# Gate/up products: a fourth of eight steps by sevens, and residual additions on GpSimd

## The chip, the cores and the metric

The kernel runs on one core of a Trainium2 chip. The metric is the device time of one execution in microseconds (us), and the median of several runs is compared. Engines are named as in the profile: PE (TensorE, matrix products; PEld is its weight load), DVE (VectorE), ACT (ScalarE), POOL (GpSimd) and SP (the queue that issues the loads).

## The reference

A two-layer decoder trunk on one sequence of 256 tokens with 2048 features. The first layer mixes tokens by causal pooling, the second by differential attention; each is followed by a SwiGLU feed-forward part with 5632 inner features. Cut to the part that the change touches:

```python
def swiglu(h, wg, wu, wd):
    return (jax.nn.silu(h @ wg) * (h @ wu)) @ wd

for i in range(DEPTH):
    hn = rmsnorm(h, norm_mix[i])
    mix = pool_mixer(...) if i % 2 == 0 else diff_attention(...)
    h = h + mix
    h = h + swiglu(rmsnorm(h, norm_ffn[i]), w_gate[i], w_up[i], w_down[i])
return rmsnorm(h, final_norm)
```

Everything is float32.

## The kernel before, in words

**A product as three.** Every float32 operand is split into a high half (a cast to the matrix type) and a low half (the rest). A product is then three matrix products of 128x128 by 128x512: high by high, high by low, low by high (lines 178 to 181).

**Groups and steps.** The 256 tokens are two blocks of 128 rows, and the weights come in groups of two column blocks of 512. A group runs over the contracted dimension in steps of 256 (two blocks of 128). So one step multiplies a 2x2 grid of blocks by a 2x2 grid of blocks. In the plain way that takes eight block products, 24 matrix products, into four banks of PSUM (C11, C12, C21, C22, which are banks M2, P3, P4 and X). In the way *by sevens* (Strassen's scheme as Winograd wrote it) it takes seven block products, 21 matrix products, into the banks M1, M2, M6, M7, P5, P3 and P4. Which of a group's steps go by sevens is written in constants: SEVEN for gate/up, SEVEN_DOWN for the down product, SEVEN_QKV and SEVEN_O for attention (lines 40 to 43). A gate/up group has eight steps, of which SEVEN names three.

**What a step costs the other engines.** `load` (L107) brings 128x2048 float32 of weights, 1 MB, through SP's queue into one of three buffers `raw`. `halves` (L112) makes `whi` (ACT) and `wlo` (DVE), of which there are three buffers as well; a step by sevens leaves out the block that it doesn't use as it is, so they are 128x1536. For a step by sevens `sums` (L119) also makes four sums of weight blocks in `tsum` (three DVE instructions), and `sum_halves` (L127) their halves `thi` (ACT) and `tlo` (DVE). Of `tsum`, `thi` and `tlo` there is one buffer each.

**Recombination.** After a group with steps by sevens, `combined` (L195) turns the eight banks into four blocks in SBUF: two ACT copies (L201, of M1, and L205, of P5) and eight DVE instructions.

**The feed-forward part.** `ffn` (L443) takes the 11 gate/up groups in chunks of 4, 4 and 3. After each gate/up group come SiLU (L463) and the product with the up half (L464), and two calls of `pair` (L245), which transpose the result block by block on PE into a bank and split it into halves, an `h` tile each. A tile for a step by sevens needs eight blocks (four of them sums, L264 to L268), an ordinary one four. After a chunk come two down groups (o = 0 and 1) over the `h` tiles of the chunk, whose result is added to the residual `x_tok` (L487, four DVE instructions of 128x512 a group). In the first layer, group 0 has one step by sevens alone.

**Banks.** There are eight. `aux` (L79) hands out banks 0 to 3 in turn for transposes; banks 4 to 7 are C12/P3, C21/P4, C11/M2 and C22/X.

**What sets the order.** The program is written as a sequence; a planner orders each engine's instructions before the run, by their place in the sequence (the priority) and by its own estimate of when operands and buffers come free. On the chip each engine goes through its list in order and waits on semaphores. The pool `hp` belongs to one layer's feed-forward part, `resid` and `const` to the whole kernel.

Of the kernel before, what the change touches and what calls it, by code (L numbers as in the profile page):

```python
# [39 lines left out]
SEVEN = (2, 4, 6)  # L40
SEVEN_DOWN = (2, 4, 6)
SEVEN_QKV = (4, 6)
SEVEN_O = (6,)

# [8 lines left out]
def trunk_kernel(ctx, tc, x_n, gains, scale_in, final_in, subln, lam_in, band, dist,  # L53
# [19 lines left out]
    turn = {"aux": 0, "of": 4}  # L73

    def bank(i, shape=(P, 512)):
        return psum.tile(list(shape), F32, name=f"b{i}", tag=f"b{i}")

# [7 lines left out]
    dist_sb = const.tile([P, 2 * P], F32, name="dist_sb")  # L85
    ident = const.tile([P, P], F32, name="ident")
    ones = const.tile([P, P], F32, name="ones")
    nc.vector.memset(ones, 1.0)
    make_identity(nc, ident)

# [9 lines left out]
    def tile_of(xp, k):  # L100
        return xp[k // 2][:, k % 2]

# [35 lines left out]
    def group(steps, pool, by_bank=0):  # L138
# [14 lines left out]
        ps = {}  # L153
# [9 lines left out]
        def products(a, seven, w, b, parts):  # L163
            first = b not in ps
            if first:
                ps[b] = bank(b)
            for at, which, block in parts:
                hi, lo = w[which]
                if seven:
                    ah, al = a[:, 0, at], a[:, 1, at]  # L170
                else:
                    k, t = at
                    if a.shape[2] == 8:
                        slot = ((A11, A21), (A12, A22))[k][t]
                        ah, al = a[:, 0, slot], a[:, 1, slot]
                    else:
                        ah, al = (a[:, k, i, t * P:(t + 1) * P] for i in range(2))
                for x, y in ((ah, hi), (ah, lo), (al, hi)):
                    left[b] -= 1
                    nc.tensor.matmul(ps[b], x, y[:, block], start=first, stop=(left[b] == 0))  # L180
                    first = False
# [13 lines left out]
    def combined(ps, pool):  # L195
# [4 lines left out]
        m1, u2, u3, p5 = (pool.tile([P, 512], F32, name=f"c{i}") for i in ("11", "12", "21", "22"))  # L200
# [44 lines left out]
    def pair(dst, src, gains, seven):  # L245

        ps = aux((P, 2, 2, P))
# [14 lines left out]
        for i, at in ((0, slice(A21, A11 + 1)), (1, slice(A22, A12 + 1, A12 - A22))):  # L262
            nc.scalar.activation(e[:, at], ps[:, i], AF.Copy, scale=1.0 if gains is None else gains[i])
        nc.vector.tensor_tensor(e[:, S1:S3 + 1], e[:, A21:A11 + 1], e[:, A22:A21 + 1], ALU.subtract)  # L264
        nc.vector.tensor_tensor(e[:, S2], e[:, S1], e[:, A11], ALU.subtract)
        nc.vector.tensor_tensor(e[:, S4], e[:, A12], e[:, S2], ALU.add)
        nc.scalar.copy(dst[:, 0], e)
        nc.vector.tensor_tensor(dst[:, 1], e, f32(dst[:, 0]), ALU.subtract)  # L268
# [11 lines left out]
    with tc.tile_pool(name="start", bufs=1, reuse_waits="tile") as st:  # L280

        warm = tmp.tile([P, 8], F32, name="warm", bufs=1)
        nc.scalar.activation(warm[:, 0:1], ones[:, 0:1], AF.Sqrt)
# [48 lines left out]
        def product(g, some):  # L332

            if some[0] == 0:
                yp[g] = [bank(4 + 2 * (g % 2) + t) for t in range(2)]
                if g >= PLAIN:
                    w_pool[g] = halves(w_pool[g])
# [76 lines left out]
    nc.sync.dma_start(out=dist_sb, in_=dist)  # L414

    def finish(cs, ys, final_sb, ss):

        for t in range(2):
            part = tmp.tile([P, 64], F32, name="part", bufs=2)
# [23 lines left out]
    def ffn(layer, xq, ss, next_op, next_gain):  # L443
# [3 lines left out]
        with tc.tile_pool(name=f"ffn{layer}", bufs=1, reuse_waits="tile") as hp:  # L447
            g0 = 0
            ys = []
            for c, n in enumerate(CHUNKS):  # L450
# [6 lines left out]
                for g in range(g0, g0 + n):  # L457

                    by_seven = SEVEN[-1:] if g == 0 and layer == 0 else SEVEN
# [5 lines left out]
                    for i in range(2):  # L465
                        at = 2 * (g - g0) + i
                        ht = hp.tile(pair_shape(at in SEVEN_DOWN), F32R, name="h", tag=f"h{at}")
                        pair(ht, lambda k, t: cs[t][1][:, (2 * i + k) * P:(2 * i + k + 1) * P], None, at in SEVEN_DOWN)
                        hp_tiles.append(ht)
                for o in range(2):  # L470
# [35 lines left out]
    with tc.tile_pool(name="attn", bufs=1, reuse_waits="tile") as ap_, ExitStack() as heads:  # L506
# [4 lines left out]
            small[:, a:b] for a, b in ((0, 2), (2, 4), (4, 8), (8, 10), (10, 12), (12, 13), (14, 16)))  # L511
        nc.sync.dma_start(out=subln_sb, in_=subln)
# [3 lines left out]

        nc.vector.tensor_tensor(lp, lam_sb[:, 0:2], lam_sb[:, 2:4], ALU.mult)
# [75 lines left out]
        for g in range(2):  # L593
            cs = scaled(combined(group([(xp[p], p in SEVEN_QKV, w_v[g, p]) for p in range(NP)], op_), op_), (r_col, r_col))
            for h in range(4 * g, 4 * g + 4):
# [13 lines left out]
                oT[h] = op_.tile(pair_shape(h in SEVEN_O), F32R, name=f"oT{h}")  # L609
# [99 lines left out]
```

## Time and profile before

| | |
|---|---|
| median of 3 runs | 1845.67 us (1845.63 to 1845.70) |
| the profiled execution, its time | 1846.21 us |
| its span, first to last instruction | 1844.4 us |
| granted TensorE clock, mean | 0.997 |
| ACT, busy | 1038.0 us, 56% of the span |
| read from memory | 353.36 MB, 193 GB/s over the span |

The page gives the busy time of each engine; the other views cut it by line and form of instruction, by stretch of time, by wait and in order of time. In a row of a timeline stand the start, the duration, the engine, the line, the operation and the tile that it writes, an arrow, and the tiles that it reads; in brackets the idle time of the engine before it and what ended that. A row of waits says who waited for whom, then the total in us, the count and the longest. A busy PE isn't PE at its peak: matrix products are pipelined, so that each shows a longer duration than the distance from its start to the next one's.

### The profile page before, as it was taken

To read this page: it belongs to the slowest core of one execution; us is meant where nothing else is said; L and a number is where in the kernel's file an instruction comes from. 1 tells how busy PE (TensorE), PEld (TensorE's weight loads), DVE (VectorE), ACT (ScalarE), POOL (GpSimd) and SP (SyncE) were. 2 spreads that over 40 slices of the span, in tenths; PEclk is the share of its full clock that TensorE was granted. 3 is DMA by queue.
4 is the path that set the end of the run, shared out by engine and by line. 5 is a ranking of instruction groups with operands and counts; after the bars stand their busy time and mean duration, and the time that the engine had idled before them with its cause. 6 is when DMAs were issued, how large, how long until landed. Compare 5 with 4: busy or idle time off the path is not lost.

```text
span 1844.4 us, 20901 instructions
## 1 busy us (share of the span) xinstructions
PE 1829.2 (99%) x8210; PEld 1495.6 (81%) x8210; DVE 1604.2 (87%) x1662; ACT 1038.0 (56%) x1006; POOL 0.7 (0%) x6
## 2 busy tenths in 40 slices
PE   9999999999999999999999999999999999999998
PEld 6788888888888888888888888788888888888886
DVE  6889998898989899988888678998989899998986
ACT  6555555555554556665566655555555555545553
POOL 0000000000000000000000000000000000000000
PEclk9999999999999999999999999999999999999999
DMA  7555555655555555555454454555555555565552
GB/s 273 183 201 187 193 210 194 210 196 194 203 198 204 202 186 183 208 180 171 173 177 164 160 188 176 205 203 187 204 205 204 188 201 183 206 227 204 206 186 111
DMA packets 50642, 356.80 MB, mean 193 GB/s; under 512 B 6000, under 2 KB 6128, under 8 KB 8048
## 3 DMA queue, kind: packets, MB, share of 16 engines
q1 hardware_dynamic: 49824, 353.85, 54.4%
q10 hardware_dynamic: 720, 1.62, 0.2%
q8 instruction: 64, 1.05, 0.2%
q14 instruction: 34, 0.28, 0.0%
HBM read 353.36 MB, written 2.10 MB: 193 GB/s over the span
## 4 chain that ended last, share of the span: by engine, by line
PE 95%; DVE 2%; ACT 1%; issue 1%; DMA 1%; SPq 0%; DVEq 0%; ACTq 0%
PE b L180 90%; PE b L250 2%; PE b L342 1%; DVE wlo L116 1%; PE b L554 1%; PE b L345 1%; PE b L584 0%; DMA w<-pool_w 0%; DMA raw<-w_gu 0%; DVE tlo L131 0%; ACT whi L115 0%; DVE tsum L121 0%; PE b L600 0%; PE b L598 0%; PE b L599 0%
## 5 line engine op out<-in xcount | busy, mean ns | idle before, releaser
L115 ACT CAST whi<-raw 128x1536 fp32r<-128x1536 f32 (+1 forms) x330 | 585.2, 1774 | 585.4 <-PE b L180 499.6
L180 PE MATMUL b<-whi,xp 128*128 128x512 f32 x2824 | 908.8, 392 | 1.2 <-DVE c L203 1.0
L116 DVE TENSOR_TENSOR wlo<-raw,whi 128x1536 fp32r<-128x1536 f32 (+1 forms) x330 | 697.3, 2113 | 193.1 <-ACT whi L115 192.9
L180 PEld LDWEIGHTS b<-whi,xp 128*128 128x128 f32 x2824 | 528.3, 188 | 110.1 <-DVE c L203 1.5
L180 PE MATMUL b<-wlo,xp 128*128 128x512 f32 x1412 | 551.8, 391 | 1.6 <-DVE wlo L116 1.6
L180 PE MATMUL b<-whi,h 128*128 128x512 f32 x1108 | 354.5, 390 | 0.0
L180 PEld LDWEIGHTS b<-wlo,xp 128*128 128x128 f32 x1412 | 265.3, 188 | 55.5 <-DVE wlo L116 1.9
L131 DVE TENSOR_TENSOR tlo<-tsum,thi 128x2048 fp32r<-128x2048 f32 x108 | 246.7, 2285 | 3.9 <-ACT thi L130 3.9
L180 PEld LDWEIGHTS b<-whi,h 128*128 128x128 f32 x1108 | 207.5, 188 | 43.1
L180 PE MATMUL b<-wlo,h 128*128 128x512 f32 x554 | 215.8, 389 | 0.0
L130 ACT CAST thi<-tsum 128x2048 fp32r<-128x2048 f32 x108 | 206.3, 1910 | 13.7 <-DVE tsum L124 13.6
L180 PE MATMUL b<-thi,xp 128*128 128x512 f32 x608 | 211.8, 390 | 0.0
L121 DVE TENSOR_TENSOR tsum<-raw 128x1024 f32<-128x1024 f32 x108 | 131.8, 1220 | 2.3 <-DMA raw<-w_v 0.6
L180 PEld LDWEIGHTS b<-thi,xp 128*128 128x128 f32 x608 | 113.9, 188 | 24.0 <-ACT thi L130 0.9
L180 PEld LDWEIGHTS b<-wlo,h 128*128 128x128 f32 x554 | 104.0, 188 | 21.3
L180 PE MATMUL b<-tlo,xp 128*128 128x512 f32 x304 | 119.5, 393 | 0.0
L180 PE MATMUL b<-thi,h 128*128 128x512 f32 x240 | 83.7, 389 | 0.0
L124 DVE TENSOR_TENSOR tsum<-tsum,raw 128x512 f32<-128x512 f32 x108 | 74.3, 688 | 2.3
L123 DVE TENSOR_TENSOR tsum<-tsum,raw 128x512 f32<-128x512 f32 x108 | 73.9, 684 | 0.6
L180 PE MATMUL b<-whi,oT 128*128 128x512 f32 x236 | 74.4, 392 | 0.0
L180 PEld LDWEIGHTS b<-tlo,xp 128*128 128x128 f32 x304 | 57.0, 188 | 16.1 <-DVE tlo L131 4.4
L180 PEld LDWEIGHTS b<-thi,h 128*128 128x128 f32 x240 | 45.1, 188 | 9.2
(147 smaller groups left out, 1192.5 us busy)
## 6 DMA issues: line engine op xcount, KB each, us to landing
raw<-w_gu SPq DMA_DIRECT2D x176, 1024.0 KB, 4.9
raw<-w_down SPq DMA_DIRECT2D x88, 1024.0 KB, 4.8
raw<-w_qk SPq DMA_DIRECT2D x32, 1024.0 KB, 4.9
raw<-w_v SPq DMA_DIRECT2D x16, 1024.0 KB, 4.8
raw<-w_o SPq DMA_DIRECT2D x16, 1024.0 KB, 4.8
raw<-pool_w SPq DMA_DIRECT2D x2, 1024.0 KB, 13.8
x_tok<-x_n SPq DMA_DIRECT2D x2, 768.0 KB, 9.0
w<-pool_w SPq DMA_DIRECT2D x2, 512.0 KB, 6.6
```

The costliest lines, as they stand in the source:

```text
L115: nc.scalar.copy(hi[:, lo_block:], raw[:, lo_block:])
L116: nc.vector.tensor_tensor(lo[:, lo_block:], raw[:, lo_block:], f32(hi[:, lo_block:]), ALU.subtract)
L121: nc.vector.tensor_tensor(t[:, T1:T3 + 1], raw[:, B11:B22 + 1], raw[:, B12:B12 + 1].broadcast_to([P, 2, 512]), ALU.add)
L123: nc.vector.tensor_tensor(t[:, T2], t[:, T1], raw[:, B22], ALU.add)
L124: nc.vector.tensor_tensor(t[:, T4], t[:, T2], raw[:, B21], ALU.add)
L130: nc.scalar.copy(hi, t)
L131: nc.vector.tensor_tensor(lo, t, f32(hi), ALU.subtract)
L180: nc.tensor.matmul(ps[b], x, y[:, block], start=first, stop=(left[b] == 0))
L250: nc.tensor.transpose(ps[:, i, 1 - t if seven else t], src(i, t), ident)
L342: nc.tensor.matmul(yp[g][t], a[:, rows], w[:, at], start=(at == 0), stop=(at == 3))
L345: nc.tensor.matmul(yp[g][t], u, v[:, at], start=(at == 0 and j == 0), stop=(at == 3 and j == 2))
L554: nc.tensor.matmul(sc[:, :nk], qk[:, 0, c, qb * P:(qb + 1) * P], qk[:, 1, c, :nk], start=True, stop=True)
```

## The change

1. SEVEN becomes (0, 2, 4, 6): half of the eight steps of a gate/up group go by sevens. Group 0 keeps what it had, in both layers.
2. The seven products of a step come in another order: M1, M2, P3, then P5, M7, M6, then P4. In a group's first step P3 comes behind M6.
3. P3 and P4 share one tile of two banks (`two_banks`), and the four recombined blocks one tile `c`. Four DVE instructions of 128x512 in `combined` become two of 128x1024.
4. Both pairs of a gate/up group use bank 7 (X) in place of two of the banks 0 to 3; the instructions on `e` of a pair by sevens are put 150 places back in the planner's priority (`behind`).
5. In down groups outside a layer's last chunk, the four DVE additions to the residual become two on GpSimd of 128x1024, 150 places back as well.
6. Constants and small tiles move to other memory (`ones`, `dist_sb`, `part`), and half of attention's `oT` tiles take the memory of `xp` tiles. The load of `dist` is issued at the beginning of attention.

```diff
-SEVEN = (2, 4, 6)
+SEVEN = (0, 2, 4, 6)
+BEHIND = 150
...
+    def two_banks():
+        both = psum.tile([P, 2, 512], F32, name="b45", tag="b45")
+        return [both[:, i] for i in range(2)], both
...
+    def behind(n):
+        return tc.high_priority(-n) if n else nullcontext()
...
             if seven:
-                plan.append([(M1, [(A11, 0, B11)]), (M2, [(A12, 0, B21)]), (M6, [(S2, 1, T2)]), (M7, [(S3, 1, T3)]),
-                             (P5, [(S1, 1, T1)]), (P3, [(S4, 0, B22)]), (P4, [(A22, 1, T4)])])
+                raw = [(M1, [(A11, 0, B11)]), (M2, [(A12, 0, B21)]), (P3, [(S4, 0, B22)])]
+                summed = [(P5, [(S1, 1, T1)]), (M7, [(S3, 1, T3)]), (M6, [(S2, 1, T2)]), (P4, [(A22, 1, T4)])]
+                late = 3 if plan else 2
+                plan.append(raw[:late] + summed[:3] + raw[late:] + summed[3:])
...
-        nc.vector.tensor_tensor(u2, p5, u2, ALU.subtract)
-        nc.vector.tensor_tensor(p5, p5, u3, ALU.subtract)
-        nc.vector.tensor_tensor(u2, ps[P3], u2, ALU.add)
-        nc.vector.tensor_tensor(u3, ps[P4], u3, ALU.add)
+        nc.vector.tensor_tensor(c[:, 1:4:2], c[:, 3:4].broadcast_to([P, 2, 512]), c[:, 1:3], ALU.subtract)
+        nc.vector.tensor_tensor(c[:, 1:3], ps["both"], c[:, 1:3], ALU.add)
...
-        ps = aux((P, 2, 2, P))
+        ps = aux((P, 2, 2, P)) if at is None else bank(at, (P, 2, 2, P))
...
+        with behind(BEHIND if at is not None else 0):
+            nc.vector.tensor_tensor(e[:, S1:S3 + 1], e[:, A21:A11 + 1], e[:, A22:A21 + 1], ALU.subtract)
+            nc.vector.tensor_tensor(e[:, S2], e[:, S1], e[:, A11], ALU.subtract)
+            nc.vector.tensor_tensor(e[:, S4], e[:, A12], e[:, S2], ALU.add)
+            nc.scalar.copy(dst[:, 0], e)
+            nc.vector.tensor_tensor(dst[:, 1], e, f32(dst[:, 0]), ALU.subtract)
...
-                    by_seven = SEVEN[-1:] if g == 0 and layer == 0 else SEVEN
+                    by_seven = SEVEN if g else SEVEN[1:] if layer else SEVEN[-1:]
...
+                    if not last:
+                        with behind(BEHIND):
+                            for t in range(2):
+                                to = x_tok[:, t, o * 1024:(o + 1) * 1024]
+                                nc.gpsimd.tensor_tensor(to, latest["c"][:, 2 * t:2 * t + 2].rearrange("p b n -> p (b n)"),
+                                                        to, ALU.add)
+                        continue
...
+        dist_sb = hq.tile([P, 2 * P], F32, name="dist_sb")
+        nc.sync.dma_start(out=dist_sb, in_=dist)
...
+                if h < 4:
+                    oT[h] = op_.tile(pair_shape(h in SEVEN_O), F32R, name=f"oT{h}")
+                else:
+                    oT[h] = resid.tile(pair_shape(h in SEVEN_O), F32R, name="xp", tag=f"xp{h}")
```

More of the change, by code (lines that the diff above doesn't have):

```diff
@@ L1 @@
 import math
-from contextlib import ExitStack
+from contextlib import ExitStack, nullcontext
 import concourse.bass as bass
@@ L152, in group @@
                 left[b] = left.get(b, 0) + 3 * len(parts)
-        ps = {}
+        ps, opened = {}, set()
         def prepared(seven, src):
@@ L163, in products @@
         def products(a, seven, w, b, parts):
-            first = b not in ps
-            if first:
+            first = b not in opened
+            opened.add(b)
+            if first and b in (P3, P4) and b not in ps:
+                (ps[P3], ps[P4]), ps["both"] = two_banks()
+            elif first and b not in ps:
                 ps[b] = bank(b)
@@ L199, in combined @@
             return [[ps[C11], ps[C12]], [ps[C21], ps[C22]]]
-        m1, u2, u3, p5 = (pool.tile([P, 512], F32, name=f"c{i}") for i in ("11", "12", "21", "22"))
+        c = latest["c"] = pool.tile([P, 4, 512], F32, name="c")
+        m1, u2, u3, p5 = (c[:, i] for i in range(4))
         nc.scalar.copy(m1, ps[M1])
@@ L243, in split, with pair @@
         nc.vector.scalar_tensor_tensor(dst[:, 1, :], src, gain, f32(dst[:, 0, :]), ALU.mult, ALU.subtract)
-    def pair(dst, src, gains, seven):
-        ps = aux((P, 2, 2, P))
+    def pair(dst, src, gains, seven, at=None):
+        ps = aux((P, 2, 2, P)) if at is None else bank(at, (P, 2, 2, P))
         for i in range(2):
@@ L260, in pair @@
         e = tmp.tile([P, 8, P], F32, name="e", bufs=1)
[L262 to L268, printed above, removed]
+        for i, to in ((0, slice(A21, A11 + 1)), (1, slice(A22, A12 + 1, A12 - A22))):
+            nc.scalar.activation(e[:, to], ps[:, i], AF.Copy, scale=1.0 if gains is None else gains[i])
+        with behind(BEHIND if at is not None else 0):
[4 more added lines that the diff above has]
+            nc.vector.tensor_tensor(dst[:, 1], e, f32(dst[:, 0]), ALU.subtract)
     def transposed(xp, j, gain, seven=()):
@@ L280, in trunk_kernel @@
     with tc.tile_pool(name="start", bufs=1, reuse_waits="tile") as st:
+        ones = st.tile([P, P], F32, name="ones")
+        nc.vector.memset(ones, 1.0)
         warm = tmp.tile([P, 8], F32, name="warm", bufs=1)
+        make_identity(nc, ident)
         nc.scalar.activation(warm[:, 0:1], ones[:, 0:1], AF.Sqrt)
@@ L334, in product @@
             if some[0] == 0:
-                yp[g] = [bank(4 + 2 * (g % 2) + t) for t in range(2)]
+                yp[g] = [bank(6 + t) for t in range(2)] if g % 2 else two_banks()[0]
                 if g >= PLAIN:
@@ L413, in trunk_kernel @@
     turn["of"] = 4
-    nc.sync.dma_start(out=dist_sb, in_=dist)
     def finish(cs, ys, final_sb, ss):
         for t in range(2):
-            part = tmp.tile([P, 64], F32, name="part", bufs=2)
+            part = tmp.tile([P, 8], F32, name="warm", bufs=1) if t == 0 else \
+                tmp.tile([P, 2, 4], F32, name="ss").rearrange("p a b -> p (a b)")
             nc.vector.tensor_reduce(part[:, 0:1], ss[:, t, 0:2], AX.X, ALU.add)
@@ L467, in ffn @@
                         ht = hp.tile(pair_shape(at in SEVEN_DOWN), F32R, name="h", tag=f"h{at}")
-                        pair(ht, lambda k, t: cs[t][1][:, (2 * i + k) * P:(2 * i + k + 1) * P], None, at in SEVEN_DOWN)
+                        pair(ht, lambda k, t: cs[t][1][:, (2 * i + k) * P:(2 * i + k + 1) * P], None, at in SEVEN_DOWN, X)
                         hp_tiles.append(ht)
@@ L515, in trunk_kernel @@
         nc.vector.tensor_scalar(qs_col, r_col, QK_SCALE, None, ALU.mult)
+        ones = hq.tile([P, P], F32, name="ones")
+        nc.vector.memset(ones, 1.0)
         nc.vector.tensor_tensor(lp, lam_sb[:, 0:2], lam_sb[:, 2:4], ALU.mult)
```

6 lines of the change are left out of this document (1 added, 5 removed).

## The prediction

> **What bounds the kernel now.** I read the head of the page, then the table of busy time by stretch, then the waits, then the timeline of VectorE (DVE) and TensorE (PE) over one gate/up group.
>
> ```profile
> span 1844.4 us, 20901 instructions
> PE 1829.2 (99%) x8210; PEld 1495.6 (81%) x8210; DVE 1604.2 (87%) x1662; ACT 1038.0 (56%) x1006; POOL 0.7 (0%) x6
> ```
>
> PE is full on average and DVE not far behind. An average says little here, so I cut the span where the recombination of a group begins (the ScalarE copy of M1). The columns are busy time and count of PE, PEld, DVE, ACT, POOL.
>
> ```profile
> 296.22:337.70 41.48, 41.48 (x185) 34.36 (x184) 37.56 (x32) 20.64 (x15) 0.00 (x0) 1.00 0.57 202
> 337.70:380.10 42.40, 42.40 (x192) 35.08 (x191) 37.67 (x32) 23.03 (x19) 0.00 (x0) 1.00 0.57 199
> 380.10:422.83 42.73, 42.73 (x192) 35.02 (x191) 38.87 (x35) 24.19 (x21) 0.00 (x0) 1.00 0.55 197
> 465.55:508.26 42.71, 42.71 (x192) 34.99 (x191) 38.87 (x35) 24.14 (x20) 0.00 (x0) 1.00 0.56 196
> 508.26:549.74 41.48, 41.48 (x184) 34.35 (x184) 37.56 (x32) 20.65 (x14) 0.00 (x0) 1.00 0.57 204
> ```
>
> In order: a down group followed by a chunk's first gate/up group; that group followed by the next; a later gate/up group followed by another; the last one followed by the down product; down to down. PE has no idle in any, so it sets the pace. But DVE is idle for only 3.9 us of each. A stretch holds five plain steps of 24 products and three by sevens of 21: 183 products. In the down stretches nothing else runs on PE, so one product costs 41.48 / 183 = 0.2267 us.
>
> ```profile
> ACT whi L115 <- PE b L180: 499.6, 224, 4.7
> DVE wlo L116 <- ACT whi L115: 192.9, 146, 4.2
> PEld b L180 <- DVE tlo L131: 6.9, 17, 0.4
> ```
>
> ScalarE waits for PE to give back a weight buffer, and DVE waits for ScalarE. DVE's idle time is thus mostly a lead, as large as three buffers allow. The third row shows where the lead is already used up: 17 times PE waits for `tlo`. One of them:
>
> ```profile
> 444.88 0.39 PE L180 MATMUL b<-whi,xp 128*128 128x512 f32 x1
> 445.26 0.50 PE L180 MATMUL b<-tlo,xp 128*128 128x512 f32 x1
> 445.59 0.40 PE L180 MATMUL b<-thi,xp 128*128 128x512 f32 x1
> ```
>
> Starts are 0.38 and 0.33 us apart in place of 0.227: a loss of 0.26 us.
>
> **Products removed.** Twenty gate/up groups (1 to 10 of both layers) get a fourth step by sevens, 3 products fewer each: 60 x 0.2267 = 13.6 us of PE. The new order puts the raw product P3 ahead of the products that need `tlo`, 3 x 0.2267 = 0.68 us more time, against a wait of 0.26 us; if DVE is no later than now, 17 x 0.26 = 4.4 us go too. Ceiling: 18.0 us.
>
> **What DVE pays.** Durations and starts:
>
> ```profile
> L116 DVE TENSOR_TENSOR wlo<-raw,whi 128x2048 fp32r<-128x2048 f32 x222 | 508.1, 2289 | 178.8 <-ACT whi L115 178.7
> L131 DVE TENSOR_TENSOR tlo<-tsum,thi 128x2048 fp32r<-128x2048 f32 x108 | 246.7, 2285 | 3.9 <-ACT thi L130 3.9
> L121 DVE TENSOR_TENSOR tsum<-raw 128x1024 f32<-128x1024 f32 x108 | 131.8, 1220 | 2.3 <-DMA raw<-w_v 0.6 <-DMA raw<-w_gu 0.2
> L487 DVE TENSOR_TENSOR x_tok<-c,x_tok 128x512 f32<-128x512 f32 x44 | 28.3, 683 | 0.0
> ```
>
> ```profile
> 425.15 0.68 DVE L202 TENSOR_TENSOR c<-b,c 128x512 f32<-128x512 f32 x1
> 425.75 1.22 DVE L121 TENSOR_TENSOR tsum<-raw 128x1024 f32<-128x1024 f32 x1
> 426.88 0.68 DVE L204 TENSOR_TENSOR c<-b,c 128x512 f32<-128x512 f32 x1
> ...
> 434.60 0.68 DVE L123 TENSOR_TENSOR tsum<-tsum,raw 128x512 f32<-128x512 f32 x1
> 435.20 1.75 DVE L116 TENSOR_TENSOR wlo<-raw,whi 128x1536 fp32r<-128x1536 f32 x1
> 436.87 0.41 DVE L264 TENSOR_TENSOR e<-e 128x256 f32<-128x256 f32 x1
> 437.21 0.68 DVE L255 TENSOR_TENSOR h<-b,h 128x512 fp32r<-128x512 f32 x1
> 437.81 0.28 DVE L265 TENSOR_TENSOR e<-e 128x128 f32<-128x128 f32 x1
> 438.01 0.68 DVE L124 TENSOR_TENSOR tsum<-tsum,raw 128x512 f32<-128x512 f32 x1
> 438.61 0.28 DVE L266 TENSOR_TENSOR e<-e 128x128 f32<-128x128 f32 x1
> 439.57 2.29 DVE L116 TENSOR_TENSOR wlo<-raw,whi 128x2048 fp32r<-128x2048 f32 x1 [0.68 <-ACT whi L115]
> 441.78 1.22 DVE L268 TENSOR_TENSOR h<-e,h 128x1024 fp32r<-128x1024 f32 x1
> 442.92 2.29 DVE L131 TENSOR_TENSOR tlo<-tsum,thi 128x2048 fp32r<-128x2048 f32 x1
> 445.12 1.75 DVE L116 TENSOR_TENSOR wlo<-raw,whi 128x1536 fp32r<-128x1536 f32 x1
> ```
>
> From start to start an instruction takes 0.08 us less than its duration: 2.20 us for 128x2048, 1.67 for 128x1536, 1.13 for 128x1024, 0.60 for 128x512. A plain step costs DVE 2.20 us; one by sevens 1.13 + 0.60 + 0.60 + 2.20 + 1.67 = 6.20, so one more adds 4.0, or 4.1 with the small stalls of dependent sums. The recombination turns two pairs of 128x512 into two of 128x1024: 2 x (1.20 - 1.13) = 0.14 us saved a group, whether the source is PSUM or not (all 128x512 rows agree). In the eight down groups that aren't in a layer's last chunk, four additions leave DVE: 2.4 us each.
>
> Beside each stretch stands what the two engines need afterwards:
>
> - Down to first gate/up (4 of the 20): DVE 37.56 + 4.1 - 0.14 - 2.4 = 39.1, PE 41.48 - 0.68 = 40.8. PE sets it: 4 x 0.68 = 2.7 us gained.
> - First gate/up to second (6): DVE 41.6, PE 41.7. Level, so I take half of 6 x 0.68: 2.0 us.
> - Later gate/up to gate/up (10): DVE 38.87 + 4.1 - 0.14 = 42.83, PE 42.73 - 0.68 - 0.26 = 41.79. **DVE becomes the bound** by 1.04 us; at its pace they last 42.83, or 0.1 us longer than now: 1.0 us lost.
> - Last gate/up to down (6): no added step, DVE has room: 6 x 0.26 = 1.6 us gained.
> - Down to down: DVE falls to 35.0 us, PE stays: nothing.
>
> A chunk begins with DVE ahead, since the down stretches leave it 4 to 6 us free. That lead is bounded by three buffers and by one `thi`/`tlo`; I let it pay half of the ten shortfalls of 1.04 us, 5.2 us (bounds 0 and 10.4). Together 2.7 + 2.0 - 1.0 + 1.6 + 5.2 = 10.5 us.
>
> **Edits without a row.** *GpSimd additions*, sixteen of 128x1024: nothing on the span waits for them, because x_tok is next touched a chunk later and c a group later. The nearest rows are DVE's 1.13 us for this shape and the only GpSimd instruction that reads a tile:
>
> ```profile
> masks.py:199 POOL TENSOR_SCALAR_AFFINE_SELECT ident<-ident 128x128 f32<-128x128 f32 x1 | 0.3, 293 | 0.1
> ```
>
> By its 293 ns for 128 columns, 1024 columns take 2.34 us. What it does to DVE beside it no row shows: bounds 0 and 16 x 2.34 us of DVE time; I take 0, with the other end as a rival. *Pairs through bank 7*: both pairs of a group now pass one bank after the other, and bank 7 is also C22 of a plain step. Between gate/up groups the first step by sevens doesn't use it, and C22 comes 39 products (8.8 us) after the group's end. Before a down group it comes 18 products (4.1 us) after. The rows below place the group's end: M1 is copied after the third product of the last step by sevens, 42 products before it, so at 422.8 + 9.5 = 432.3.
>
> ```profile
> 422.81 0.58 ACT L201 COPY c<-b 128x512 f32<-128x512 f32 x1
> 434.42 0.38 PE L250 MATMUL b<-ident,c 128*128 128x128 f32 x2
> 435.63 0.66 ACT L263 ACTIVATE e<-b 128x256 f32<-128x256 f32 x2 [2.11 <-PE b L250]
> 436.17 0.59 ACT L254 CAST h<-b 128x512 fp32r<-128x512 f32 x1
> ```
>
> The first pair is read out at 436.3; then the second needs its transposes (0.4), its copy (0.59) and DVE's L255 (0.68): 438.0, 5.7 us after the end against 4.1. That is 1.6 us, six times, or 9.6; nothing if the planner sets the next step's products ahead, as it does with the `thi` products ahead of `tlo`. I take 2 us, nearer to nothing. *One addition for P3 and P4*: before a plain first step it has 12 products (2.7 us) from P4's end to P3's reuse, where each had 18; a `wlo` in front (2.20) and 1.13 of its own miss that by 0.6 us, some 20 times: bounds 0 and 12, taken 1. *Deferred halves of a pair*: their 1.9 us of DVE remain in the sum, only later; the h tile isn't read until the down product. *dist, ones, oT in other memory*: the small loads already stand on SP's queue at this place, behind five loads of the weights that follow; one more changes nothing: 0. *xq[0] by sevens* turns two pairs, one in the pooling stage and one in the output projection, into 1.9 us of DVE from about 0.8, where DVE has room: 0.
>
> ```profile
> 730.35 18.52 SPq L109 DMA_DIRECT2D raw<-w_qk  x5
> 748.92 0.42 SPq L512 DMA_DIRECT2D small<-subln  x1
> ```
>
> Forecast: 10.5 - 2 - 1 = 7.5 us less than the profiled execution's 1846.2, which stands 0.5 above the median of the three runs: 1838.2, so **1838**.
>
> **A rule against it.** The Trainium skill (SBUF — State Buffer, "Who interferes with whom") says that a VectorE instruction with two SBUF inputs and a GpSimd instruction that reads SBUF shut each other out, whichever starts second. No row here can show it, as GpSimd reads nothing beside DVE; by it the third rival would decide and the sum would end at about 1847.
>
> **Rivals.**
> 1. *PE keeps the end throughout.* The lead covers all shortfalls: the ceiling of 18.0, **1828**. For it: 3.9 us of DVE idle in every stretch. Against: 42.83 is more than 41.79, and `tlo` is late today.
> 2. *DVE as the bound keeps part of its idle, slower.* Place: the sixteen gate/up stretches that follow a gate/up group. The 0.68 us before the `wlo` at 439.57 isn't lead: ScalarE itself is late there. With x us of such idle a stretch and no lead, ten cost 0.1 + x and six x - 0.75 each, against 4.3 gained elsewhere; it decides from x = 0.5, and x = 1.1 gives 12.0 + 2.1 - 4.3 = 9.8 us more: **1855**.
> 3. *GpSimd and DVE shut each other out.* Two additions of 2.34 us after a down group hold DVE for 4.7. Down to down has the room (35.0 + 4.7 below 41.48). Down to first gate/up has not: 43.8 against 40.8, four times 3.0 = 12 us; the lead takes some 3 of it: **1847**.
> 4. *Bank 7 holds C22 before the down product*, at 9.6 in place of 2: 1838.2 + 7.6, **1846**.
>
> **How the numbers follow.** Chances: forecast (1834 to 1842) 0.40; rival 1 0.17; rival 2 0.18; rival 3 0.15; rival 4 0.10. A measurement can tell 0.2%, 3.7 us, from no change. Faster: 0.38 + 0.17 + 0.02 of rival 3 = 0.57. Within: 0.02 of the forecast, 0.11 of rival 3, 0.09 of rival 4 = 0.22. Slower: 0.18 + 0.02 + 0.01 = 0.21. The range of 8 in 10 goes from rival 1, 1828, past rivals 3 and 4 to 1851, and leaves most of rival 2 out. The forecast's own range is 1834 to 1842.
>
> **What would show it.** Right: 7488 products at L180's place; stretches of 40.8 after a down group, 41.7 to 42.4 after a chunk's first group, near 42.4 later, with DVE idle under 0.5 us in the later ones and PE's waits all on `tlo` or `wlo`. Rival 1: waits on `tlo` under 1 us in all. Rival 2: later stretches over 43 us, with DVE idle for ScalarE. Rival 3: `wlo` or `tlo` rows of over 4 us beside POOL. Rival 4: PE waiting in a chunk's first down group for the DVE reads of bank 7. I am wrong if a gate/up step by sevens costs DVE other than 4 us more than a plain one, or if DVE's idle turns out not to be lead.

## The result and the profile after

The changed kernel takes 1920.45 us (median of 4 runs, 1918.06 to 1920.74) against 1845.68 us (4 runs, 1845.63 to 1845.84) on the same chip: 1.0402 times as long, with a 95% interval of 1.0384 to 1.0420. It is slower by 74.8 us, where 7.5 us less was forecast.

The head of its page, with the busy time of each engine, and the summary of the chain that ended last:

```profile
span 1918.6 us, 20788 instructions
...
PE 1850.1 (96%) x8150; PEld 1483.6 (77%) x8150; DVE 1693.1 (88%) x1633; ACT 1058.7 (55%) x1028; POOL 42.5 (2%) x22
...
PE 74%; DVE 14%; issue 5%; ACT 5%; DMA 2%; SPq 0%; ACTq 0%; DVEq 0%
```

There are 60 matrix products fewer (8150 for 8210), and yet PE is busy longer, and 4% of the span it is not busy at all. The chain now passes through DVE and ACT for a fifth of the span. DVE is busy for 89 us more than before, and still idle for 12% of the span. To see where the time went, I cut both traces at the first matrix product of each group. Mean length of a stretch in us, by the kinds that the prediction used:

| stretch (number) | before | forecast | after | difference in all |
|---|---|---|---|---|
| down to first gate/up (4) | 41.48 | 40.8 | 45.90 | +17.7 |
| first gate/up to second (6) | 42.52 | 42.2 | 43.91 | +8.3 |
| later gate/up to gate/up (10) | 42.73 | 42.8, less a lead | 47.19 | +44.6 |
| last gate/up to down (6) | 39.37 | 39.1 | 39.85 | +2.9 |
| down to down (5) | 39.78 | the same | 39.80 | +0.1 |

Together 73.6 us. The groups of attention, the first group of each layer and the last of all gave 3.2 us back, and some 4 us more lie ahead of the first group and behind the last. So nearly all of it lies in the gate/up groups that got a fourth step by sevens. The table by stretch for three of them, in order a later one, a first one after a down group, another later one (length, then busy time and count of PE, PEld, DVE, ACT and POOL, then the clock):

```profile
133.60:178.68 45.08, 43.19 (x189) 34.11 (x188) 41.59 (x36) 24.82 (x20) 0.00 (x0) 1.00 0.53 187
310.67:356.55 45.88, 43.14 (x182) 34.74 (x180) 40.83 (x31) 22.88 (x15) 5.23 (x2) 0.96 0.42 146
446.80:495.10 48.30, 44.07 (x190) 33.95 (x189) 43.90 (x39) 25.63 (x20) 0.00 (x0) 1.00 0.57 204
```

The price of DVE's work was about right: in the ten later stretches DVE is busy for 43.28 us in the mean (41.5 to 44.6), where 42.83 was forecast. What is wrong is the idle time beside it. DVE is idle for 3.5, 5.1 and 4.4 us in the three rows, and for 3.91 us in the mean of the ten (2.5 to 5.2), where it was 3.86 before; and now PE waits, for results of DVE and ACT.

Where in a group this happens shows when the third stretch is cut at its steps: steps 0 and 1, steps 2 to 6, step 7. The first three rows are the same group in the kernel before, the others in the kernel after:

```profile
431.00:442.83 11.83, 11.83 (x57) 9.74 (x56) 11.15 (x15) 8.02 (x8) 0.00 (x0) 1.00 0.49 173
442.83:468.28 25.45, 25.45 (x112) 20.76 (x111) 22.27 (x16) 13.95 (x10) 0.00 (x0) 1.00 0.59 209
468.28:473.72 5.44, 5.44 (x25) 4.50 (x24) 5.44 (x7) 2.20 (x2) 0.00 (x0) 1.00 0.57 193
446.82:461.73 14.91, 12.66 (x55) 9.09 (x53) 14.91 (x16) 7.67 (x8) 0.00 (x0) 1.00 0.49 160
461.73:487.68 25.95, 25.50 (x112) 20.35 (x110) 21.55 (x18) 15.62 (x11) 0.00 (x0) 1.00 0.55 204
487.68:495.09 7.41, 5.88 (x24) 4.50 (x25) 7.41 (x7) 2.34 (x2) 0.00 (x0) 1.00 0.78 294
```

Steps 2 to 6 last about what they did, and all of DVE's idle time lies there. The loss lies at the seam of two groups, steps 7, 0 and 1: DVE is busy in all of it, with the recombination, the products behind SiLU and the pairs beside the weights, and PE is idle for 3.8 us. The ten stretches are alike in this. Summed over them, the seams last 213.9 us for 172.8, with 29.5 of PE's 31.5 us of idle time and only 2.0 of DVE's 39.2; steps 2 to 6 last 258.0 us for 254.5. So 41.1 of the 44.6 us lie at the seam. The waits of the whole kernel (who for whom, total, count, longest):

```profile
ACT whi L120 <- PE b L190: 368.3, 162, 5.4
ACT thi L135 <- DVE tsum L129: 166.3, 62, 5.1
DVE wlo L121 <- ACT whi L120: 107.1, 90, 4.2
DVE tlo L136 <- ACT thi L135: 69.9, 43, 2.3
ACT whi L120 <- DMA raw<-w_gu: 52.5, 35, 4.6
...
PE b L190 <- DVE tlo L136: 25.5, 19, 2.1
```

ACT's wait for `tsum` was 13.6 us before (29 times):

```profile
ACT thi L130 <- DVE tsum L124: 13.6, 29, 4.0
```

DVE and PE are hardly ever idle together (0.1 us in the ten stretches): DVE is idle first, and PE waits for it afterwards. How that comes about stands in the timeline of the end of the third stretch, ACT first, then DVE, then PE (start, duration, engine, line, tile; in brackets the idle time before):

```profile
483.91 1.91 ACT L120 CAST whi<-raw 128x2048 fp32r<-128x2048 f32 x1 [4.33 <-PE b L190]
485.73 1.91 ACT L135 CAST thi<-tsum 128x2048 fp32r<-128x2048 f32 x1
...
483.05 0.69 DVE L129 TENSOR_TENSOR tsum<-tsum,raw 128x512 f32<-128x512 f32 x1
485.86 2.29 DVE L121 TENSOR_TENSOR wlo<-raw,whi 128x2048 fp32r<-128x2048 f32 x1 [2.12 <-ACT whi L120]
488.06 2.28 DVE L136 TENSOR_TENSOR tlo<-tsum,thi 128x2048 fp32r<-128x2048 f32 x1
...
487.68 1.19 PE L190 MATMUL b<-thi,xp 128*128 128x512 f32 x4 [0.46 <-ACT thi L135]
490.40 0.50 PE L190 MATMUL b<-tlo,xp 128*128 128x512 f32 x1 [1.53 <-DVE tlo L136]
```

ACT has stood idle for 4.33 us, first in its list being a `whi` whose buffer PE still uses. DVE finishes `tsum` at 483.74. By then the `thi` that PE needs next could start, but the `whi` is ahead of it in ACT's list, and so is its `wlo` ahead of `tlo` in DVE's. DVE waits 2.12 us for that `whi`, makes the `wlo`, and only then the `tlo` for which PE waits.

### The profile page after: what moved, and what is told of

It reads as the page before. It is cut to its first block, busy times and chain, and to the rows that moved or that the text cites. A ratio compares the mean times of both kernels' runs of the same rounds, so it can differ in the third digit from the quotient of the medians.

```text
span 1918.6 us, 20788 instructions
## 1 busy us (share of the span) xinstructions
PE 1850.1 (96%) x8150; PEld 1483.6 (77%) x8150; DVE 1693.1 (88%) x1633; ACT 1058.7 (55%) x1028; POOL 42.5 (2%) x22
## 4 chain that ended last, share of the span: by engine, by line
PE 74%; DVE 14%; issue 5%; ACT 5%; DMA 2%; SPq 0%; ACTq 0%; DVEq 0%
PE b L190 70%; DVE wlo L121 4%; ACT whi L120 3%; DVE tlo L136 2%; PE b L259 1%; DVE tsum L126 1%; ACT thi L135 1%; DVE c L217 1%; DVE tsum L129 1%; DMA raw<-w_gu 1%; DVE c L218 1%; DVE c L214 1%; DVE c L215 1%; PE b L578 1%; DVE c L213 1%
## 5 line engine op out<-in xcount | busy, mean ns | idle before, releaser
L190 PE MATMUL b<-whi,xp 128*128 128x512 f32 x2732 | 883.5, 393 | 7.6 <-ACT whi L120 4.6
L136 DVE TENSOR_TENSOR tlo<-tsum,thi 128x2048 fp32r<-128x2048 f32 x128 | 292.8, 2287 | 70.8 <-ACT thi L135 69.9
L135 ACT CAST thi<-tsum 128x2048 fp32r<-128x2048 f32 x128 | 244.4, 1910 | 178.6 <-DVE tsum L129 166.3
L190 PE MATMUL b<-thi,xp 128*128 128x512 f32 x784 | 272.3, 405 | 8.2 <-ACT thi L135 7.8
L190 PEld LDWEIGHTS b<-thi,xp 128*128 128x128 f32 x784 | 146.4, 192 | 51.7 <-ACT thi L135 24.4
L190 PE MATMUL b<-tlo,xp 128*128 128x512 f32 x392 | 160.1, 408 | 25.5 <-DVE tlo L136 25.5
L126 DVE TENSOR_TENSOR tsum<-raw 128x1024 f32<-128x1024 f32 x128 | 155.9, 1218 | 2.7 <-DMA raw<-w_v 1.5
L129 DVE TENSOR_TENSOR tsum<-tsum,raw 128x512 f32<-128x512 f32 x128 | 101.1, 789 | 1.5
L128 DVE TENSOR_TENSOR tsum<-tsum,raw 128x512 f32<-128x512 f32 x128 | 89.4, 698 | 0.7
L501 POOL TENSOR_TENSOR x_tok<-c,x_tok 128x1024 f32<-128x1024 f32 x16 | 41.8, 2632 | 1668.9 <-DVE c L218 1668.9
L476 ACT ACTIVATE c<-c,r_tok 128x512 f32<-128x512 f32 x44 | 31.8, 722 | 39.9 <-DVE c L214 23.0
```

Source lines behind the costliest of these rows:

```text
L126: nc.vector.tensor_tensor(t[:, T1:T3 + 1], raw[:, B11:B22 + 1], raw[:, B12:B12 + 1].broadcast_to([P, 2, 512]), ALU.add)
L128: nc.vector.tensor_tensor(t[:, T2], t[:, T1], raw[:, B22], ALU.add)
L129: nc.vector.tensor_tensor(t[:, T4], t[:, T2], raw[:, B21], ALU.add)
L135: nc.scalar.copy(hi, t)
L136: nc.vector.tensor_tensor(lo, t, f32(hi), ALU.subtract)
L476: nc.scalar.activation(gate, gate, AF.Silu, scale=r[:, t:t + 1])
```

## The experiments

The theories. **Lists**: each engine's order is fixed before the run, and the chain `tsum`, `thi`, `tlo` changes engine three times, so DVE's idle time is bound to places where it waits for ACT; a fourth chain adds its 4 us to a group that keeps its idle. **Load**: DVE simply has too much to do. **Place**: it is step 0 by sevens, next to step 6 of the group before and to the recombination. **Buffers**: more buffers would turn idle time into lead. And the other edits: GpSimd, the order of products, the deferral. Times are single runs where no interval is given; the kernel before took 1845.4 to 1846.0 us beside them.

### One edit undone at a time

Three steps by sevens, all other edits kept:

```diff
-SEVEN = (0, 2, 4, 6)
+SEVEN = (2, 4, 6)
...
-                    by_seven = SEVEN if g else SEVEN[1:] if layer else SEVEN[-1:]
+                    by_seven = SEVEN[-1:] if g == 0 and layer == 0 else SEVEN
```

> The changed kernel with three steps by sevens a gate/up group, as before; all its other edits stay. Theory A (the fourth step is too much for the loop from PE over ACT and DVE back to PE): the gate/up groups that follow a gate/up group fall from 44 to 49 us to 42.4 or so; what stays is the stall behind the GpSimd additions, four gate/up groups at 2 to 4 us over, 1846 to 1862. Theory B (the other edits - product order, pairs on one bank, deferral - make the stalls): the gate/up groups stay over 44 us, 1900 or more.

Measured 1866.22 us: 54.2 of the 74.8 us are the fourth step's, although it saves 60 products. The other edits cost 20.8 us without it. The later stretches fall to 42.59 us.

The additions to the residual back on DVE:

```diff
-                    if not last:
-                        with behind(BEHIND):
...
-                        continue
```

> The changed kernel with the residual additions back on DVE, four of 128x512 a down group. If GpSimd and DVE shut each other out (a sum of 0.68 us shows 2.58, a wlo of 1.75 shows 3.96, beside each pair of additions), these two rows go back to 0.68 and 1.75, and the four gate/up groups that follow a down product fall from 45.9 us to 41 to 43: 12 to 20 us less, 1900 to 1908. If that is only a place where DVE would have been late anyhow, they fall by less than 2 us each, and the whole stays at 1912 to 1920.

Measured 1930.67 us, 10.2 more: with four steps by sevens, GpSimd is the better place, whatever it costs. The slow rows that the expectation names are gone, but neither of its times came.

No deferral:

```diff
-BEHIND = 150
+BEHIND = 0
```

> The changed kernel with the deferral taken out (0 places in place of 150). Theory A: DVE gets the halves of a pair earlier, in the tightest place; tlo is later there and the kernel slower than 1920 by 0 to 15 us. Theory B with the deferral as its cause: under 1900.

Measured 1928.28 us, 7.8 more. The deferral isn't the loss.

The old order of the products:

```diff
-                raw = [(M1, [(A11, 0, B11)]), (M2, [(A12, 0, B21)]), (P3, [(S4, 0, B22)])]
...
+                plan.append([(M1, [(A11, 0, B11)]), (M2, [(A12, 0, B21)]), (M6, [(S2, 1, T2)]), (M7, [(S3, 1, T3)]),
+                             (P5, [(S1, 1, T1)]), (P3, [(S4, 0, B22)]), (P4, [(A22, 1, T4)])])
```

> The changed kernel with the seven products in the order of before (M1, M2, M6, M7, P5, P3, P4). Theory A: PE needs tlo 0.68 us earlier in a step, about 80 such steps, so slower than 1920 by 5 to 30 us. Theory B with the new order as its cause (P3, P4 and the sums come late for the recombination): under 1900.

Measured 1924.63 us, 4.2 more. With four steps by sevens, none of the other three edits is by itself the loss; each helps a little, the order by hardly more than the four runs of the kernel after differ (2.7 us).

### Three steps by sevens, additions on DVE

The first two edits together:

> Three steps by sevens and the residual additions on DVE: the changed kernel without its two large parts; product order, joined additions, pairs on one bank and deferral stay. With three steps by sevens and GpSimd, the two groups behind each down product took 44.4 and 44.4 us, the one between two down products 42.3 to 42.6. If that was the exclusion of GpSimd and DVE, they return to 41.5, 42.4 and 41.5, and the whole is at 1842 to 1850. If the pairs on one bank or the joined additions did it, it stays at 1860 to 1867.

Measured 1858.62 us, 7.6 less than with the additions on GpSimd (1866.22). The stretches after a down group show it: 42.03 us against 43.67, four times 1.64, is 6.6 of the 7.6. What GpSimd does there stands in the timeline of the kernel after (POOL, then DVE):

```profile
315.09 5.23 POOL L501 TENSOR_TENSOR x_tok<-c,x_tok 128x1024 f32<-128x1024 f32 x2 [38.36 <-DVE c L218]
...
313.13 0.68 DVE L128 TENSOR_TENSOR tsum<-tsum,raw 128x512 f32<-128x512 f32 x1
...
315.46 2.59 DVE L129 TENSOR_TENSOR tsum<-tsum,raw 128x512 f32<-128x512 f32 x1
317.98 6.16 DVE L121 TENSOR_TENSOR wlo<-raw,whi 128x1536 fp32r<-128x1536 f32 x2
324.06 2.28 DVE L136 TENSOR_TENSOR tlo<-tsum,thi 128x2048 fp32r<-128x2048 f32 x1
```

The two `wlo` stand in one row; the view by tile takes them apart (shortest, median and longest in ns):

```profile
L121 DVE TENSOR_TENSOR wlo<-raw,whi x2: 2277/3117/3957, 318.0 to 321.9; 128x1536 fp32r<-128x1536 f32 x1, 128x2048 fp32r<-128x2048 f32 x1
```

A sum of 0.68 us takes 2.59 beside POOL, and a `wlo` of 128x1536, 1.75 us elsewhere, takes 3.96. That is 1.91 + 2.21 = 4.1 us of DVE for each pair of additions; once POOL is done, the `tlo` has its usual 2.28. All eight pairs of additions show two such rows; with the additions on DVE no such sum takes over 0.69 us and no such `wlo` over 1.76. This is the exclusion that the Trainium skill (SBUF — State Buffer, "Who interferes with whom") describes, and the trace agrees.

With three steps by sevens and DVE's additions, the kernel still loses 12.8 us to the kernel before. Its page is nearly that of before:

```profile
PE 1832.8 (99%) x8210; PEld 1491.5 (80%) x8210; DVE 1600.6 (86%) x1581; ACT 1022.2 (55%) x1006; POOL 0.7 (0%) x6
```

### How much of DVE's work must go

The kernel after, with the low half of the weights left out in steps 1 and 5 of the gate/up groups from the second on: the products use the high half in its place, so PE's work is the same and DVE has two `wlo` fewer, 4.4 us a group. Then the same in step 3 alone, 2.2 us a group.

```diff
-    def halves(raw, lo_block=0):
+    def halves(raw, lo_block=0, skip=False):
         hi = whl.tile([P, 4, 512], F32R, name="whi")
-        lo = whl.tile([P, 4, 512], F32R, name="wlo")
         nc.scalar.copy(hi[:, lo_block:], raw[:, lo_block:])
+        if skip:
+            return hi, hi
+        lo = whl.tile([P, 4, 512], F32R, name="wlo")
```

> The changed kernel, but steps 1 and 5 of the gate/up groups make no low half of their weights; their high-by-low products use the high half once more, so PE has the same products and DVE 4.4 us less a group, about what the fourth step by sevens added. Theory A1 (DVE has too much work): gate/up groups behind a gate/up group fall from 44 to 49 us to 41.8 to 43. Theory A2 (the single thi and tlo, passed from PE to ACT to DVE and back, are the loop): they stay over 44.

> The changed kernel with the low half of the weights left out in step 3 alone of the gate/up groups from 1 on (high half used once more): 2.2 us of DVE less a group, 40.6 us in the later ones. Theory L: PE sets their pace, 41.8 to 42.3 us, the whole 1848 to 1860. Theory S: 40.6 + 3.5 to 4.4 = 44.1 to 45.0 us, 1880 to 1895.

Measured 1848.17 us without two, 1896.14 without one: 72.3 and 24.3 us less. The same stretches as above, without two:

```profile
135.04:176.91 41.87, 41.87 (x189) 34.34 (x188) 38.94 (x36) 25.44 (x20) 0.00 (x0) 1.00 0.53 201
303.14:345.75 42.61, 41.10 (x182) 33.72 (x180) 39.24 (x29) 22.84 (x15) 5.76 (x2) 1.00 0.54 201
429.39:471.23 41.84, 41.84 (x190) 34.32 (x188) 37.89 (x34) 23.85 (x19) 0.00 (x0) 1.00 0.51 187
```

These two later stretches reach the 41.8 us that were worked out for PE, and the mean of the ten is 42.09. So the products' saving is real once DVE has two `wlo` less to make. Yet DVE's idle time isn't used even so: with one `wlo` left out, the ten last 45.07 us in the mean, with DVE busy for 40.3 and idle for 4.8.

### Does the place of the step matter

Three steps by sevens with step 0 among them, additions on DVE (layer 1's first group has one step by sevens fewer there, 3 products more):

```diff
-SEVEN = (0, 2, 4, 6)
+SEVEN = (0, 2, 4)
```

> Three steps by sevens a gate/up group as in g1_three_dve (additions on DVE), but steps 0, 2 and 4 in place of 2, 4 and 6; layer 1's group 0 has two (3 products more in all). DVE's work is that of g1_three_dve, 38.9 us a group; steps 6, 7 are plain, so the single thi and tlo are long free at step 0. Theory M (the seam: a step by sevens right behind the group's end meets the recombination, SiLU and the pairs, which DVE has to do in the same few us): 1 to 3 us lost in steps 0 and 1 of each later group, 1875 to 1910. Theory T (DVE's total with four steps by sevens): no loss there, 1857 to 1863.

and the same with (0, 4, 6):

> The same with steps 0, 4 and 6. Step 6 and the next group's step 0 are now only a plain step apart, with one buffer each of thi and tlo. Theory M with the buffers in it: more lost in steps 0 and 1 than with 0, 2 and 4, by 1 us or more a group. If the seam is DVE's work alone: as with 0, 2 and 4. Theory T: 1857 to 1863 for both.

Measured 1857.37 and 1868.79 us. The later stretches last 42.62 and 42.61 us, as with (2, 4, 6): with three steps in all, neither step 0 by sevens nor step 6 close ahead of it loses anything there. So place alone isn't the cause in the ten stretches that cost most. But it is where the work of a fourth step ends up: with three, steps 7, 0 and 1 keep DVE busy for 16.1 to 17.3 us a stretch, whichever three they are, and PE hardly waits there; with four they keep it busy for 21.2. By itself the place costs time behind a down group, where step 0 falls on the recombination and four additions: 43.94 and 46.67 us, against 42.03 without step 0.

### Is DVE's idle time needed

The kernel before, with additions of 128x512 on DVE that nobody uses, three in each gate/up group from the second on, or seven (as much as a fourth step by sevens costs), or seven close behind the start of the group:

```diff
+            if n in more:
+                extra = tmp.tile([P, 512], F32, name="sq", bufs=1)
+                nc.vector.tensor_tensor(extra, x_tok[:, 0, 0:512], x_tok[:, 1, 0:512], ALU.add)
```

> The same with three additions, behind steps 1, 3 and 5: 1.8 us of DVE a group. Theory L: no change, 1845 to 1847, since 40.7 us is well under 42.7. Theory S: 40.7 + 3.5 to 4.4 = 44.2 to 45.1 us in the later groups, 1865 to 1895.

> The kernel before, with seven more DVE additions of 128x512 that nobody uses in each of the twenty gate/up groups from 1 on, one behind the weights of each of the first seven steps: 7 x 0.60 = 4.2 us of DVE a group, as much as the fourth step by sevens brought, but no other buffer, wait, ACT work or product. If DVE's idle of 3.9 us a group is a lead that can be spent (theory L, the prediction's), DVE needs 43.1 us in the later gate/up groups against 42.7 now: 1846 to 1852. If the idle stays whatever DVE has to do (theory S), these groups take 43.1 + 3.5 to 4.4 = 46.6 to 47.5 us and the whole 1890 to 1930.

> The kernel before with the seven unused DVE additions of i1_more7, but four behind the weights of step 0 and three behind those of step 1 in place of one behind each step. Same DVE work, 4.2 us a group. Theory M as a matter of DVE's work alone: 1 to 3 us lost in steps 0 to 2 of a gate/up group, 1875 to 1905. If what a seam can't take is the step by sevens with its chain over ACT and its buffers, not DVE's work as such: 1855 to 1870, as with the even spread (1860).

Measured 1846.30, 1860.37 and 1859.53 us. The page of the kernel with seven:

```profile
PE 1836.6 (99%) x8210; PEld 1492.0 (80%) x8210; DVE 1681.0 (90%) x1802; ACT 1033.9 (56%) x1006; POOL 0.7 (0%) x6
```

DVE does 77 us more than before, nearly the 89 us of the change, and the time rises by 14 us, not 75. But these totals don't decide between load and lists, because the planner moved the additions: of the 140, only 24 are in the ten later stretches, ten of them in one, and with three a group none of the 60 is. What can be compared are single stretches: the later one with ten additions, a later one with none, and one after a down group with six:

```profile
1227.10:1270.01 42.91, 42.84 (x192) 34.70 (x191) 42.67 (x43) 23.21 (x18) 0.00 (x0) 1.00 0.56 192
434.43:477.96 43.53, 43.08 (x192) 34.82 (x191) 39.18 (x37) 24.09 (x20) 0.00 (x0) 1.00 0.57 197
307.09:349.13 42.04, 41.91 (x184) 34.39 (x184) 41.80 (x41) 20.95 (x14) 0.00 (x0) 1.00 0.54 193
```

Where such work is, it uses the idle time up: with ten additions DVE is filled to 42.67 of 42.91 us, near the 43.28 of the kernel after, and the stretch lasts 0.2 us longer than before, where work by sevens made it last 4.5 longer. That is one stretch of the ten. Where there are none, DVE keeps 3.8 to 4.4 us of idle time.

### Buffers

As a base for more buffers, shorter chunks and one step by sevens in the down groups free 16 KB of each partition. The page counts 8195 matrix products there for 8150, 45 more, and not the 48 that the expectation below says:

```diff
-CHUNKS = (4, 4, 3)
+CHUNKS = (3, 3, 3, 2)
-SEVEN_DOWN = (2, 4, 6)
+SEVEN_DOWN = (2,)
```

> A control for the next: the changed kernel with chunks of 3, 3, 3 and 2 gate/up groups in place of 4, 4 and 3, and one step by sevens a down group in place of two or three, which frees 16 KB a partition. 30 steps by sevens of the down products become 14, 48 products more (11 us). Gate/up groups behind a gate/up group as in the changed kernel, 44 to 48 us.

Measured 1899.75 us. On it, in the feed-forward part, two buffers each of `thi` and `tlo`:

> The control with two buffers each of thi and tlo. Theory A2 (the single buffers are the loop): the gate/up groups behind a gate/up group fall by 2 us or more against the control, the whole by 25 to 50. Theory A1 (DVE has too much work): DVE needs 42.8 us a group whatever the buffers, and has idle only by waits; less than 1 us a group, under 15 in all.

then a fourth pair of `whi` and `wlo`, and then five `raw` in place of three:

> The kernel of h1_chunks (1899.75) with a fourth pair of buffers for the halves whi and wlo, in the feed-forward part alone (every fourth step uses a pair from its pool). Theory A, three pairs of halves are what keeps DVE's idle time from becoming lead: gate/up groups behind a gate/up group fall to DVE's 42.8 us, the kernel to 1850 to 1865. Theory B, each engine's fixed order and the chain tsum, thi, tlo through ScalarE keep it: within 10 us of 1899.75, as with two buffers of thi and tlo (1893.59). Theory C, late loads (raw): no change here either, but a gain in l5_raw5.

> The kernel of h1_chunks (1899.75) with five raw weight buffers in place of three in the feed-forward part. Theory C, weights that arrive when a buffer comes free, and so late, set the loss (ScalarE waited 52.5 us for loads in the profile after, none to speak of before): 1850 to 1875, and ScalarE's wait for loads goes. Theory A or B: the waits for loads go, but the time stays within 10 us of 1899.75, since whi then waits for PE or for its turn instead.

Measured 1893.59, 1917.95 and 1903.00 us: 6 us less, 18 more, 3 more. With five `raw` buffers ACT's wait for gate/up loads, 30.7 us in the base,

```profile
ACT whi L120 <- DMA raw<-w_gu: 30.7, 26, 2.7
```

is gone, and only a sum on DVE still waits for them:

```profile
DVE tsum L129 <- DMA raw<-w_gu: 7.1, 6, 1.5
```

Yet the last gate/up group of a chunk lasts what it did: 45.69 us in the base, 45.69 with five (the second chunk's in the first layer). There late loads were a consequence. Elsewhere they did cost time: with five `raw` the stretches behind a down group fall from 42.21 to 40.80 us and the second groups from 42.25 to 41.83, 12 us in all, which longer first groups (50.80 for 45.84) and 7.6 us more in attention outweigh. Two buffers of `thi` and `tlo` take the later stretches from 45.70 to 44.38 us and the second groups from 42.25 to 43.50. With a fourth pair of halves that last group takes 50.71 us; the planner wrote another order for it, so this run tells less. None of the three kinds of buffer gave the idle time of the later stretches back: it is 3.4 us a stretch in the base, and 3.6, 6.5 and 3.4 with more buffers.

### The order of the products, alone

On the kernel before, the new order everywhere; and P3 ahead of the products that need sums in gate/up groups alone (timed in 5 runs):

```diff
...
+                p3 = [(P3, [(S4, 0, B22)])]
+                plan.append((raw + p3 + summed if raw_first else raw + summed + p3) + [(P4, [(A22, 1, T4)])])
```

> The kernel before with the new order of the seven products alone. If P3 ahead of the sums gives tlo the 0.68 us that it lacks by 0.26, the 17 waits go: 1840.5 to 1842. If the recombination, which gets M6, M7 and P5 later, runs into the next group's banks, 1846 to 1855.

> The kernel before with one edit, in gate/up groups alone: P3 moved ahead of M6, M7, P5, so that tlo has 0.68 us more. The 17 waits of 0.26 us go: 1841 to 1842. In j1_order the gate/up groups behind a gate/up group fell from 42.73 to 42.45 us, but down groups lost 0.3 to 0.9; if that comes from the gate/up groups in front of them, 1845 to 1850.

Measured 1853.08 us, and 1853.17 (1.0040 times the kernel before, 95% interval 1.0026 to 1.0055). In the ten later stretches the wait for `tlo` is gone: 42.48 us for 42.73, the 0.26 us of the prediction. The other stretches pay: after a down group 42.12 for 41.48, first to second 42.84 for 42.52, to the down product 39.66 for 39.37, down to down 40.41 for 39.78. With the counts of the table these are -2.5, +2.6, +1.9, +1.7 and +3.2 us: 6.9 of the 7.4 measured. The planner writes another order for ACT, in a later group with the first `thi` ahead of a `whi` where it stood behind it, and ACT's waits for `tsum` rise to 267.0 us:

```profile
ACT thi L130 <- DVE tsum L124: 267.0, 71, 5.4
```

It also shows that this total alone is no measure of a loss: it is larger here than in the kernel after, at 67 us less time.

No kernel that computes the whole result beat the kernel before.

## Why the prediction was wrong

**The step that failed** is "DVE's idle time is thus mostly a lead", and with it the price of the later stretches, "at its pace they last 42.83", and the lead that was to "pay half of the ten shortfalls". DVE's work of 42.83 us was sized well (43.28 in the mean of the ten), but the idle time was not lead that could be spent. It stayed at 3.91 us a stretch, so that they last 47.19 in the mean: 44.6 us lost where 1.0 was to be lost and 5.2 won. The prediction weighed DVE against PE over whole stretches. Most of the idle time lay in steps 2 to 6, and the fourth step's work came on top at the seam, steps 7, 0 and 1, where DVE had only 0.7 us a stretch to spare before: there it is busy for 21.2 us in place of 16.6, and PE waits. One reading was off as well, without weight here: the second of the five rows by stretch leaves DVE 4.7 us of idle time, not 3.9.

**Why the idle time stays.** The runs show what it isn't by itself: not the amount of DVE's work (42.67 us fit into the one later stretch with ten unused additions), not step 0 nor its distance from step 6 (42.6 us with both), not the number of buffers of `thi` and `tlo` or of the weights (of `whi` and `wlo` less surely). What DVE waits for has changed: before, 37.3 of its 38.6 us of idle time in the ten stretches were for `whi`; now 18.5 of 39.2 are for `whi` and 17.4 for `thi`. What is left is the order of the lists. The trace after has 40 chains of `thi` and `tlo` in the ten stretches, and PE waits amid the products of 18 of them, for 28.0 us. In eight, all at step 6, `thi` stands behind a `whi` that waits for PE, as at 483 to 490 us (10.5 us of PE's waits). In the other ten, all at step 0, PE waits in turn for `thi`, `whi`, `tlo`, the recombination and the pairs, while DVE works without a pause (17.6 us). So the lists are seen to hold DVE back at step 6; at steps 0 and 1 it is full. Why its idle time in steps 2 to 6 can't take over the work of the seam, and how much another order would give back, stays open: no kernel was tried that differs from the kernel after in the order of these lists alone.

**Products removed**: right. 41.8 us in eight of the ten later stretches, as worked out, where DVE is relieved of two `wlo`. **The wait for `tlo`**: right in its place, 0.25 us a stretch against 0.26, but the new order that removes it was put at nothing elsewhere and costs 9.4 us in other stretches, so that it loses 7.4 by itself.

**After a down group** 40.8 was forecast and 45.90 came. Two mechanisms meet there: the exclusion (1.64 us a stretch with three steps by sevens), and step 0 by sevens on top of the recombination, which costs 1.9 to 4.6 us even with the additions on DVE (43.94 and 46.67 against 42.03). In the kernel after, the loss lies in step 2, just behind GpSimd's additions, where PE waits for `tlo` (8.1 of its 10.9 us of idle time in the four stretches) and its clock falls once in each. Taking GpSimd away from the kernel after doesn't help (46.47): DVE then has the additions themselves, and PE waits for `thi` in step 0 (12.1 us in the four).

**First to second gate/up**: taken as "Level", 42.2; 43.91 came. With three steps by sevens it was 43.95 and 43.96, but the wait is another. With four, PE waits for `tlo` (6.2 us in the six stretches). With three, step 0 is plain, and PE waits for the joined addition L218 (6.0 us; with the additions on DVE 1.8, and 4.0 for a `wlo`): the term "One addition for P3 and P4", which was taken at 1 with 12 as its bound. With three steps of which step 0 is one, these stretches last 42.78 and 42.57. For the kernel with three, after GpSimd's 7.6 us and the order's 7.1 to 7.4, about 6 of the 20.8 us of the other edits are left; their place is this stretch, six times 1.1 us over the kernel with the order alone (43.96 against 42.84). What the deferral and the shared bank 7 have to do with it was not separated.

**The rivals.** *Rival 2* came closest: right in its place and in its mechanism, DVE as the bound that keeps its idle time, but with x at 4.4 us in the later stretches (47.19 less 42.83; 3.9 of it idle time, 0.45 more work) where 1.1 was taken. By its own sum the ten cost 10 x (0.1 + 4.4) = 45 us, which is what they did. It had set x too low because it took for bound only the one wait of 0.68 us at 439.57, and for lead the rest of the 3.9. *Rival 3* was right in its mechanism: `wlo` of 4.0 us beside POOL, 4.1 us of DVE for two additions, against 4.7 taken. GpSimd's own price was 2.34 forecast, 2.63 measured in the mean:

```profile
L501 POOL TENSOR_TENSOR x_tok<-c,x_tok 128x1024 f32<-128x1024 f32 x16 | 41.8, 2632 | 1668.9 <-DVE c L218 1668.9
```

*Rival 4*, bank 7 ahead of the down product, was to show 1.6 us a group; with three steps by sevens, which keep bank 7 for both pairs, these stretches are shorter than before (39.15 against 39.37). It falls. *Rival 1* is what the relieved kernel shows in its later stretches, and no more than that.

## What to carry to other kernels

An engine's idle time is lead only if the work to be added can be done whenever the engine is free: ask of each new instruction what it waits for, and in which list that stands behind what. Weigh the two engines step by step and not only stretch by stretch: here most of the idle time lay in the middle of a group and the new work came at its ends. A cheap test ahead of such a change is to add the same amount of unused work that waits for nobody, and then the same amount in the chain's own form; here they cost 14 and 54 us. Look where the first went before comparing: here most of it lay in other stretches, because work that waits for nobody can also be moved by the planner. When two engines are both near their limit and hand work to each other, the bound of a stretch is not the larger of their busy times but that plus the hand-overs, and an order that removes one wait is paid for in others.

## What the runs showed of the hardware

Six times in the kernel after, within 1.5 us of a wait of PE of 1.5 to 2.1 us, its clock went to half for 3.4 us. The table by stretch has it for the place behind the 2.06 us wait, and the timeline of PE shows the wait itself, the longest of the 14 us ahead:

```profile
327.40:330.80 3.40, 3.40 (x9) 2.63 (x8) 3.40 (x3) 1.39 (x1) 0.00 (x0) 0.51 0.36 147
```

```profile
321.99 0.50 PE L190 MATMUL b<-wlo,xp 128*128 128x512 f32 x1 [0.68 <-DVE wlo L121]
326.39 0.50 PE L190 MATMUL b<-tlo,xp 128*128 128x512 f32 x1 [2.06 <-DVE tlo L136]
```

Products stand 0.43 us apart there in place of 0.227, so a drop costs about 1.7 us; the six cost at most some 10 us of the 74.8. Four lie in the stretches after a down group. The length of the wait alone doesn't decide: two waits of 1.53 us in the same trace, and waits of 2.04 to 2.07 us in the kernel without the deferral, had no drop behind them. The Trainium skill (TensorE: Matmul & The Clock Gate, "Part 1: The HAM clock gate") puts the fall to half rate after an idle window of about 3.4 us; here waits of 1.5 to 2.1 us stood ahead of the drops, and the length of the drop, 3.4 us, agrees with its window. It isn't the cause of the loss: the kernel without the deferral has a granted clock of 0.997 and takes 1928.28 us.
